# A gate branch through DRAM, the last convolution taps in a later stage, a fused mask and row maximum, and a plain unit between keys and values

## The chip, the cores and the metric

The kernel runs on one core of one Trainium2 chip. The metric is device time in microseconds (us) of one execution, the median of several runs; lower is better. The engines are named as in the profile: PE multiplies matrices (PEld loads its weights), DVE and ACT work on vectors, POOL is used here for small work and for issuing DMAs, and SP issues the DMAs of the weights. PE writes to PSUM, which has eight banks; everything else lies in SBUF or in DRAM. Each engine works through its own queue in order.

## The reference

One decoder layer on 256 tokens with 2048 channels, in float32. Two mixers run side by side on the same normalised input: causal attention with 16 heads on compressed queries, keys and values, and a short convolution over three tokens. Each is widened by a SiLU gate and projected back; the two are merged by sigmoid gates and projected once more.

```python
h = _rmsnorm(x, pre_norm_g)
(q_a, c_kv, k_rope, z_mla, c_in, b_gate, c_gate, z_conv, g_mla, g_conv) = split(h @ w_in)
q = _rmsnorm(q_a) @ w_q_b ; k_nope, v = split(_rmsnorm(c_kv) @ w_kv_b)   # 16 heads, rope on q and k
attn = softmax(causal(q k) * scale) v
y_mla = (attn * silu(z_mla)) @ w_o_mla
u = c_gate * c_in
conv = sum(conv_w[k] * u_pad[:, k:k + s] for k in range(3))
y_conv = (b_gate * conv * silu(z_conv)) @ w_o_conv
merged = sigmoid(g_mla) * y_mla + sigmoid(g_conv) * y_conv
out = x + _rmsnorm(merged @ w_out, post_norm_g)
```

The normalisation of x is taken out of the products: they run on x times its gain, and a factor r per token (`r_col`) is applied where a result leaves PSUM.

## The kernel before, in words

**Splitting.** To keep float32 accuracy every operand is split in a high part, rounded to the fast matmul type, and a low part, the remainder; a product is then three matmuls (`product`, L252: high by high, high by low, low by high). Weights come as units of 1 MB (128 partitions x 2048 values) into three `raw` buffers (SP issues them, L159). `split_unit` (L168) splits a unit: ACT writes the high part `whi` (L268), DVE subtracts it and writes the low part `wlo` (L269). There are three buffers of each. `take(i)` hands unit i to PE; `ahead` (L227) splits one unit further and loads three further. All units stand in one list, `plan` (L108 to L147), in the order in which PE takes them; the order of the attention stage is written out by hand twice, once for the list (L127 to L139) and once in the loop over the heads (L834 to L881), and both must agree.

**Order of the stages on PE.** First the compressed queries and keys (`qa`, `ckv`, `kr`). Then the attention stage: a loop over 16 heads, with 48 plain units (`fill`, L699) laid between the heads' steps. A plain unit is 24 matmuls of 128x512; four of them make one 512-wide column block of c_gate, c_in or z_mla (`cv` in PSUM), in the order of FILLS (L1157). Per group of two heads there is a key group "a" (`group_a`, L581: PE makes `qn` and `kn`, `whole`, L418, adds the two halves of a bank into `f`, and this is split) and a rope group "r"; per four heads there is one value group "v" (`group_v`, L601, `vv` in PSUM). The banks tagged "mm" are four, and qn, kn, qr and vv take them in turn, so a vv product waits until the `f` of an older one has been read out. At heads 5, 9 and 13 (`h > 1 == at`, the second head of a four) the order on PE is: scores, a plain unit, the key group, the value group, a plain unit, the values of the head before.

**Softmax** (`scores`, L616). The scores stand in one bank. DVE adds two halves (L636) and the causal mask (L637 and L638), takes the row maxima (L643), ACT takes the exponentials, DVE scales them and transposes 32x32 blocks; the rest of the transposition goes through DRAM by POOL's DMAs (`turned`, L344: `go` writes in four transfers, `come` reads back).

**The convolution taps** (`taps`, L750). Once a column block j of u = c_gate * c_in is done (L714, in `cv_f`), a generator works on it in three steps: POOL's DMAs bring copies shifted by one and two tokens (`mv`) and the rows of conv_w spread over the partitions (`cw`); DVE multiplies and adds (L758), first for the second half of the tokens, then for the first. Its steps are taken at `step()` (L737) in the loop over the heads; the last block, j = 3, takes them at the end of the attention stage.

**The gate blocks** (`block`, L913). Eight blocks of eight units compute z_conv (blocks 0 and 1), b_gate (2 and 3), g_mla (4 and 5) and g_conv (6 and 7); BLOCKS (L1158) gives the order. A unit is "whole", 8 products of 3 matmuls, or "pair". A pair takes two row blocks k and k + 4, both token halves and both column halves as a 2 x 2 by 2 x 2 block product with 7 products in place of 8. For this DVE and ACT make sums of the weights and split these too (`split_pair`, L202); the sums on the side of x are made once (`token_sums`), for three pairs. PLACES (L1159) says at which of the eight unit positions of each block a pair stands. At a block's end four results leave PSUM: for z_conv a sum and a SiLU into `cv_w`; for b_gate (`b_done`, L978) a sum and a multiplication by r and `cv_w`, in place; for the merge gates (`g_done`, L989) a sum, a sigmoid and a DMA to DRAM (`gate_far`), from where they are read back when they are needed.

**The projections** (`tokens`, L1029). Two products of 16 units each, first of the attention branch and then of the convolution branch, and then the output product of 16 units (`out`). During the first one `channels_steps(i)` (L1014) runs with unit i: it multiplies one 128x512 tile of the convolution by the tile of `cv_w` (L1020), starts its transposition, brings back the one of two steps before, and splits that of five steps before into `cv_both`, the operand of the second projection.

`tc.keep_in_program_order` pins an operation behind the operation traced before it on its engine; other operations may be moved in an engine's queue when the program is built.

Of the kernel before, what the change touches and what calls it, by code (L numbers as in the profile page):

```python
# [11 lines left out]
F32 = mybir.dt.float32  # L12
# [72 lines left out]
def tile_layer(ctx: ExitStack, tc: tile.TileContext, xw, x, pos, pvec, post_g, wc, wz, wcv, wkr, wqk, wqr, wv, cwr, wsq, wg, out):  # L85
# [43 lines left out]
    for h in range(H):  # L129
        at = h % HV  # L130
        order += ["fill"] + made[h] + [("v", h // HV)] * (h > 1 == at) + ["fill"] * (1 + (h > 0 and not h > 1 == at))
    for u in order:
# [483 lines left out]
    def scores(h):  # L616
# [19 lines left out]
        nc.vector.tensor_tensor(p[:, :P], sc[:, :P], half[:, :], op=ALU.add)  # L636
        nc.vector.tensor_tensor(p[:, :P], p[:, :P], mask[:, :P], op=ALU.add)  # L637
        nc.vector.tensor_tensor(p[:, P:], sc[:, S:], mask[:, P:], op=ALU.add)  # L638
        mx, sm, rs = temp("mx", (P, NT)), temp("sm", (P, NT)), temp("rs", (P, NT))
        nb = temp("nb", (P, NT))  # L640
        for t in range(NT):
            o = slice(t * P, (2 * t + 1) * P)
            nc.vector.reduce_max(mx[:, t : t + 1], p[:, o], axis=mybir.AxisListType.X)  # L643
        nc.vector.tensor_scalar(nb[:, :], mx[:, :], -SCALE, None, op0=ALU.mult)
# [54 lines left out]
    def fill(between=None):  # L699

        f = len(filled)
        filled.append(f)
        (j, n), i = FILLS[f // 4], f % 4
        if i == 0:
            cv_ps["now"] = [bank(f"cv{f}_{t}", tag="cv", bufs=2) for t in range(NT)]
        quarter(cv_ps["now"], take(u_fill[f]), i, between)
        if i < 3:
            return
        for t in range(NT):
            ps, r, u = cv_ps["now"][t], r_col[:, t : t + 1], cv_t[:, j, t, :]  # L710
            if n == 0:
                nc.scalar.activation(u, ps[:, :], AF.Copy, scale=r)
            elif n == 1:
                nc.vector.scalar_tensor_tensor(u, ps[:, :], r, u, op0=ALU.mult, op1=ALU.mult)  # L714
            else:
                nc.scalar.activation(z_now[:, t, :], ps[:, :], AF.Silu, scale=r)
        if n == 1:
            steps = taps(j)
            tap_steps.extend([steps] * 3 if j == 3 else [steps, None, steps, None, steps])
        elif n == 2:  # L720
            z_steps.append(gates_turn())
# [27 lines left out]

    def taps(j):  # L750

# [7 lines left out]

        cws = [temp("cw", (P, 512), bufs=3)[:, :] for _ in range(3)]  # L760
        for t in (1, 0):
            u, parts = cv_t[:, j, t, :], []
            for d in (1, 2):
                m = temp(f"mv{d}", (P, 512), bufs=1, tag=f"mv{d}x")
                if t:
                    bring(m[:d, :], cv_t[P - d :, j, 0, :])
                else:
                    tc.keep_in_program_order(nc.gpsimd.memset(m[:d, :], 0.0))
                bring(m[d:, :], u[: P - d, :])
                parts.append(m[:, :])  # L770
# [63 lines left out]
    for h in range(H):  # L834
# [3 lines left out]
        if h < H - 1:  # L838
            score(h)
        if h:  # L840
            fill()
# [5 lines left out]
        step()  # L847
        for i in made[h]:
            make(*i)
        if h > 1 == at:  # L850
            make("v", v)
            pt = turn(ps_by_head.pop(h - 1))
        if h == H - 3:
            lstack.close()
            d0 = dstack.enter_context(tc.tile_pool(name="d0", bufs=1))
            sums = token_sums(d0)
            xs = next(sums)
# [119 lines left out]

    def b_done(b):  # L978
        def done(ps, other, t, half):
            o = D // 2 * b + 512 * half  # L980
            w = spool["w"][:, t, o : o + 512]
            nc.vector.tensor_tensor(other, ps, other, op=ALU.add)
            nc.vector.scalar_tensor_tensor(w, other, r_col[:, t : t + 1], w, op0=ALU.mult, op1=ALU.mult)

        return done

    gate_far = {}

    def g_done(n, b):  # L989
        def done(ps, other, t, half):  # L990
            c = 2 * b + half
            g = spool["pool"].tile([P, 512], F32, name=f"sg{n}{c}{t}", tag="sg", bufs=4)
            nc.vector.tensor_tensor(g[:, :], ps, other, op=ALU.add)
            nc.scalar.activation(g[:, :], g[:, :], AF.Sigmoid, scale=r_col[:, t : t + 1])
            gate_far[n, c, t] = dram.tile([P, 512], F32, name=f"gate{n}{c}{t}", tag=f"gate{n}{c}{t}", bufs=1)
# [5 lines left out]
    for n, (name, b) in enumerate(BLOCKS):  # L1001
        put = g_done(*divmod(b, 2)) if name == "g" else {"zc": zc_done, "b": b_done}[name](b)
        if n == len(BLOCKS) - 1:
# [7 lines left out]

    channels_come = {}

    def channels_steps(i):  # L1014

        if i < 8:
            j, t = divmod(i, NT)
            u = cv_t[:, j, t, :]
            w = spool["w"][:, t, 512 * j : 512 * j + 512]
            tc.keep_in_program_order(nc.vector.tensor_tensor(u, u, w, op=ALU.mult))  # L1020
            go, channels_come[i] = turned(u, spool["pool"].tile([P, 512], F32, name="via_c", tag="via", bufs=2)[:, :], 4)
            go()
# [135 lines left out]
BLOCKS = [("zc", 0), ("zc", 1), ("b", 0), ("b", 1), ("g", 0), ("g", 1), ("g", 2), ("g", 3)]  # L1158
PLACES = [(4,), (0, 2, 4), (0, 2, 4), (0, 3), (0, 3)] + [(0, 2, 4)] * 3  # L1159

# [117 lines left out]
```

## Time and profile before

| | us |
|---|---|
| median of 3 runs | 1027.55 (1026.85 to 1028.34) |
| the profiled execution | 1027.61 |
| its span | 1025.6 |
| DVE, busy | 777.9 |
| ACT, busy | 536.5 |
| POOL, busy | 191.5 |

How to read it: the span runs from the first to the last instruction, and the execution's own time has a little more around it. The profile's page gives the busy time of each engine and the costliest groups of instructions. A line number such as L269 is one of kernel.py and can be that of a helper, so that one line stands for many places. In a row of a group the numbers behind the bar are the busy time of all its instructions in us, the mean of one in ns, and the idle time of the engine just before them with what ended it. The chain that ended last gives start, length and what was done. In a row of the windows, engines stand in the order PE, PEld, DVE, ACT, POOL, with their instructions in brackets, then the granted clock of PE, the share of the DMA engines and what they moved. In a timeline the number before an engine's name is a length, and the bracket at the end is the engine's idle time before it and what it waited for.

By the chain, PE starts its first matmul at 9.78 us, the loop over the heads ends at 422.13, the eight gate blocks end at 756.73, the two projections at 930.81, and the output product follows.

### The profile page before, as it was taken

The numbers are of one execution on the slowest core, as the hardware profiler recorded it, in microseconds if no ns is written. First come the engines' busy times: TensorE is split into PE (matmuls) and PEld (weight loads), VectorE is DVE, ScalarE is ACT, GpSimd is POOL, SyncE is SP. The second block draws the span as 40 slices with busy tenths as digits, with TensorE's granted clock in tenths as the row PEclk, the third lists the DMA queues.
The fourth block names the chain that finished last, engine by engine and source line by source line (L and its number), as shares of the span: only waits on it lengthen the run. The fifth ranks groups of instructions, "written<-read, shape, count | busy, mean of one in ns | idle before, by whom it ended". The sixth has DMA issues, their size and how long they took to land.

```text
span 1025.6 us, 12524 instructions
## 1 busy us (share of the span) xinstructions
PE 1014.0 (99%) x4634; PEld 844.6 (82%) x4634; DVE 777.9 (76%) x972; ACT 536.5 (52%) x667; POOL 191.5 (19%) x365
## 2 busy tenths in 40 slices
PE   9999999999999999999999999999999999999996
PEld 7888888788888888888888888888888888888885
DVE  7578787887879887898888788898877655656562
ACT  7756655565566664545544446555653433344451
POOL 7630321331213222220000000000024301322000
PEclk9999999999999999999999999999999999999999
DMA  8755684677666765775565556666678856777742
GB/s 324 303 192 199 227 250 180 218 249 260 222 221 202 259 217 199 259 246 212 184 216 197 202 205 221 231 237 217 234 258 300 312 217 211 271 267 243 310 165 82
DMA packets 43548, 236.25 MB, mean 230 GB/s; under 512 B 7840, under 2 KB 8544, under 8 KB 20576
## 3 DMA queue, kind: packets, MB, share of 16 engines
q1 hardware_dynamic: 29808, 197.54, 53.9%
q0 software_dynamic: 13248, 34.63, 10.7%
q10 hardware_dynamic: 432, 3.29, 0.8%
q8 instruction: 36, 0.59, 0.2%
q14 instruction: 24, 0.20, 0.1%
HBM read 215.53 MB, written 15.73 MB: 225 GB/s over the span
## 4 chain that ended last, share of the span: by engine, by line
PE 98%; DMA 1%; DVE 1%; ACT 0%; SPq 0%; issue 0%; DVEq 0%
PE g L90 33%; PE cv L90 26%; PE sq L90 17%; PE out L90 8%; PE vv L90 2%; PE kn L90 2%; PE qn L90 2%; PE ckv L90 2%; PE qa L90 2%; PE sc L90 1%; PE qr L90 1%; PE o L90 1%; DMA raw<-xw_dram 1%; PE kr L90 0%; DVE og L1132 0%; SPq L159 0%
## 5 line engine op out<-in xcount | busy, mean ns | idle before, releaser
L269 DVE TENSOR_TENSOR wlo<-raw,whi 128x1024 fp32r<-128x1024 f32 (+2 forms) x238 | 375.3, 1595 | 162.5 <-ACT whi L268 161.8
L268 ACT ACTIVATE whi<-raw 128x1024 fp32r<-128x1024 f32 (+2 forms) x240 | 316.6, 1346 | 296.9 <-PE sq L90 95.2
L90 PE MATMUL g<-whi,x_both 128*128 128x512 f32 x784 | 251.2, 389 | 0.0
L90 PE MATMUL cv<-whi,x_both 128*128 128x512 f32 x768 | 242.9, 390 | 0.0
L90 PEld LDWEIGHTS g<-whi,x_both 128*128 128x128 f32 x784 | 147.1, 188 | 30.4
L90 PEld LDWEIGHTS cv<-whi,x_both 128*128 128x128 f32 x768 | 144.2, 188 | 29.4
L90 PE MATMUL g<-wlo,x_both 128*128 128x512 f32 x392 | 152.5, 389 | 0.0
L90 PE MATMUL cv<-wlo,x_both 128*128 128x512 f32 x384 | 149.7, 390 | 0.0
L355 POOL DMA_DIRECT2D far<-via x96 | 52.8, 556 | 213.7 <-DVE via L348 160.0
L90 PEld LDWEIGHTS g<-wlo,x_both 128*128 128x128 f32 x392 | 73.6, 188 | 15.4
L90 PEld LDWEIGHTS cv<-wlo,x_both 128*128 128x128 f32 x384 | 72.2, 188 | 13.9
L90 PE MATMUL sq<-whi,x_both 128*128 128x512 f32 x256 | 79.0, 389 | 0.0
L90 PE MATMUL sq<-whi,cv_both 128*128 128x512 f32 x256 | 79.0, 389 | 0.0
L90 PE MATMUL out<-whi,x_both 128*128 128x512 f32 x256 | 79.0, 389 | 0.0
L996 POOL DMA_DIRECT2D gate<-sg x16 | 8.7, 542 | 306.3 <-PE g L90 185.0
L212 ACT ACTIVATE whi<-raw 128x1536 fp32r<-128x1536 f32 x20 | 29.8, 1491 | 61.7 <-PE g L90 44.4
L90 PEld LDWEIGHTS sq<-whi,x_both 128*128 128x128 f32 x256 | 48.0, 188 | 10.1
L90 PEld LDWEIGHTS sq<-whi,cv_both 128*128 128x128 f32 x256 | 48.0, 188 | 10.1
L90 PEld LDWEIGHTS out<-whi,x_both 128*128 128x128 f32 x256 | 48.0, 188 | 10.0
L210 DVE TENSOR_TENSOR wlo<-raw,whi 128x2048 fp32r<-128x2048 f32 x20 | 45.8, 2292 | 7.5 <-ACT whi L216 7.5
L90 PE MATMUL sq<-wlo,x_both 128*128 128x512 f32 x128 | 49.8, 389 | 0.0
L90 PE MATMUL sq<-wlo,cv_both 128*128 128x512 f32 x128 | 49.8, 389 | 0.0
(239 smaller groups left out, 1394.6 us busy)
## 6 DMA issues: line engine op xcount, KB each, us to landing
raw<-wg_dram SPq DMA_DIRECT2D x64, 1024.0 KB, 4.8
raw<-wsq_dram SPq DMA_DIRECT2D x48, 1024.0 KB, 5.2
raw<-wcv_dram SPq DMA_DIRECT2D x32, 1024.0 KB, 5.1
raw<-wz_dram SPq DMA_DIRECT2D x16, 1024.0 KB, 4.9
raw<-wqk_dram SPq DMA_DIRECT2D x8, 1024.0 KB, 4.8
raw<-wc_dram SPq DMA_DIRECT2D x4, 1024.0 KB, 10.0
raw<-wv_dram SPq DMA_DIRECT2D x4, 1024.0 KB, 4.8
gate<-sg POOLq DMA_DIRECT2D x16, 256.0 KB, 2.7
```

The source lines that it names most:

```text
L90: return tc.keep_in_program_order(nc.tensor.matmul(*a, **kw))
L210: tc.keep_in_program_order(nc.vector.tensor_tensor(*a, op=op))
L212: nc.scalar.activation(hi[:, 512:], t[:, 512:], AF.Copy)
L268: a = nc.scalar.activation(hi, src, AF.Copy)
L269: b = nc.vector.tensor_tensor(lo, src, hi.bitcast(F32), op=ALU.subtract)
L355: tc.keep_in_program_order(nc.gpsimd.dma_start(out=f[i], in_=m))
L996: tc.keep_in_program_order(nc.gpsimd.dma_start(out=gate_far[n, c, t][:, :], in_=g[:, :]))
```

## The change

- **b_gate.** `b_done` goes. The sums of blocks 2 and 3 leave as those of the merge gates do, without the sigmoid, to DRAM. In the first projection `branch_tile(i)` reads them back one step ahead (two buffers), and `channels_steps` multiplies each tile of the convolution by b_gate and r before it multiplies by `cv_w`.
- **Last taps.** The taps of column block 3 are no longer taken in the loop over the heads, but at steps 0, 2 and 4 of the first projection, with buffers of their own.
- **Mask and maximum.** One operation adds the mask and takes the row maximum.
- **Keys, plain unit, values.** At heads 5, 9 and 13 the key group comes before the first plain unit and the value group behind it; the list of units has the same order. `step()` comes behind that key group.
- **PLACES.** Blocks 3 and 4 have three paired units each in place of two.

```diff
@@ the list of units
-        order += ["fill"] + made[h] + [("v", h // HV)] * (h > 1 == at) + ["fill"] * (1 + (h > 0 and not h > 1 == at))
+        if h > 1 == at:
+            order += made[h] + ["fill", ("v", h // HV), "fill"]
+        else:
+            order += ["fill"] + made[h] + ["fill"] * (1 + (h > 0))
@@ scores
-        nc.vector.tensor_tensor(p[:, :P], p[:, :P], mask[:, :P], op=ALU.add)
-        nc.vector.tensor_tensor(p[:, P:], sc[:, S:], mask[:, P:], op=ALU.add)
-        for t in range(NT):
+        for t, src in enumerate((p[:, :P], sc[:, S:])):
             o = slice(t * P, (2 * t + 1) * P)
-            nc.vector.reduce_max(mx[:, t : t + 1], p[:, o], axis=mybir.AxisListType.X)
+            nc.vector.tensor_tensor_reduce(p[:, o], src, mask[:, o], 1.0, MASKED, ALU.add, ALU.max, mx[:, t : t + 1])
@@ fill
-            steps = taps(j)
-            tap_steps.extend([steps] * 3 if j == 3 else [steps, None, steps, None, steps])
+            steps = taps(j, bp) if j < 3 else None
+            if j < 3:
+                tap_steps.extend([steps, None, steps, None, steps])
@@ taps: its buffers come from the pool that is handed in
-    def taps(j):
+    def taps(j, pool):
-        cws = [temp("cw", (P, 512), bufs=3)[:, :] for _ in range(3)]
+        cws = [pool.tile([P, 512], F32, name=f"cw{d}", tag="cw", bufs=3)[:, :] for d in range(3)]
-                m = temp(f"mv{d}", (P, 512), bufs=1, tag=f"mv{d}x")
+                m = pool.tile([P, 512], F32, name=f"mv{d}", tag=f"mv{d}x", bufs=1)
@@ the loop over the heads
         if h < H - 1:
             score(h)
+        if h > 1 == at:
+            make(*made[h][0])
         if h:
             fill()
...
         step()
-        for i in made[h]:
-            make(*i)
         if h > 1 == at:
             make("v", v)
             pt = turn(ps_by_head.pop(h - 1))
+        else:
+            for i in made[h]:
+                make(*i)
@@ the ends of the gate blocks (b_done is deleted)
             nc.vector.tensor_tensor(g[:, :], ps, other, op=ALU.add)
-            nc.scalar.activation(g[:, :], g[:, :], AF.Sigmoid, scale=r_col[:, t : t + 1])
+            if n != "b":
+                nc.scalar.activation(g[:, :], g[:, :], AF.Sigmoid, scale=r_col[:, t : t + 1])
-        put = g_done(*divmod(b, 2)) if name == "g" else {"zc": zc_done, "b": b_done}[name](b)
+        put = zc_done(b) if name == "zc" else g_done("b", b) if name == "b" else g_done(*divmod(b, 2))
@@ ahead of the first projection
-    channels_come = {}
+    channels_come, b_come = {}, {}
+
+    def branch_tile(i):
+        w = spool["pool"].tile([P, 512], F32, name=f"b{i}", tag="b", bufs=2)
+        tc.keep_in_program_order(nc.gpsimd.dma_start(out=w[:, :], in_=gate_far[("b", *divmod(i, NT))][:, :]))
+        b_come[i] = w[:, :]
+
+    branch_tile(0)
+    tp = main.enter_context(tc.tile_pool(name="tp", bufs=1))
+    last_taps = taps(3, tp)
@@ channels_steps(i)
+        if i < 7:
+            branch_tile(i + 1)
+        if i in (0, 2, 4):
+            next(last_taps)
         if i < 8:
             j, t = divmod(i, NT)
-            u = cv_t[:, j, t, :]
+            u, r = cv_t[:, j, t, :], r_col[:, t : t + 1]
             w = spool["w"][:, t, 512 * j : 512 * j + 512]
+            tc.keep_in_program_order(nc.vector.scalar_tensor_tensor(u, b_come.pop(i), r, u, op0=ALU.mult, op1=ALU.mult))
             tc.keep_in_program_order(nc.vector.tensor_tensor(u, u, w, op=ALU.mult))
@@
-PLACES = [(4,), (0, 2, 4), (0, 2, 4), (0, 3), (0, 3)] + [(0, 2, 4)] * 3
+PLACES = [(4,)] + [(0, 2, 4)] * 7
```

More of the change, by code (lines that the diff above doesn't have):

```diff
@@ L976, in zc_done @@
         return done
[L978 to L985, printed above, removed]
     gate_far = {}
```

## The prediction

> **What bounds the kernel now.** I read the page first, then the waits of PE, then the chain of work that ended last in order of time, and after that the other engines stage by stage. The page gives the engines' shares, and PE's only wait inside the kernel's steady part follows it:
>
> ```profile
> PE 1014.0 (99%) x4634; PEld 844.6 (82%) x4634; DVE 777.9 (76%) x972; ACT 536.5 (52%) x667; POOL 191.5 (19%) x365
> ```
> ```profile
> PE vv L90 <- DVE f L422: 2.2, 2, 1.9
> ```
>
> PE works for nearly the whole span, so it sets the time and only two things can shorten it: fewer matmuls, or the removal of that 2.2 us. DVE at 76% is next, but its share is an average; where it runs full it can make PE wait. The same chain in order of time (start, length, what) shows both the price of a matmul and where PE lost time:
>
> ```profile
> 197.89 2.70 PE kn L90 x16
> 201.08 1.11 DVE wlo L269
> 202.19 0.34 DVE f L422
> 202.57 5.75 PE vv L90 x24
> 208.33 5.44 PE cv L90 x24
> ...
> 285.49 2.79 PE kn L90 x16
> 288.29 5.47 PE vv L90 x24
> 293.75 5.44 PE cv L90 x24
> ...
> 370.92 2.70 PE kn L90 x16
> 379.75 5.44 PE cv L90 x24
> ...
> 422.13 334.60 PE g L90 x1476
> 756.73 174.08 PE sq L90 x768
> ```
>
> From the last two rows: 334.60 / 1476 and 174.08 / 768 are both 0.2267 us for a 128x512 matmul, without a pause in the eight gate blocks ("g") or in the two projections ("sq"). In the other rows the values' matmuls ("vv") follow a group's keys ("kn") three times. From the start of kn to the start of the plain unit behind vv PE took 208.33 - 197.89 = 10.44 us at head 5, 293.75 - 285.49 = 8.26 us at head 9, and 379.75 - 370.92 = 8.83 us at head 13. Head 9 is undisturbed: 2.79 + 5.47 us. Heads 5 and 13 lost 2.18 and 0.57 us, together 2.75 us (more than the 2.2 us of the wait, since PE also restarts its pipeline). At head 5 the chain runs through DVE in these microseconds: a weight split (wlo, L269) stands in DVE's queue ahead of the sum f (L422) that empties the bank which vv is to take.
>
> **Part 1: two more paired units.** PLACES gives blocks 3 and 4 three paired units each in place of two. A paired unit has 7 products of 3 matmuls, a whole one 8 of 3, so 2 x 3 = 6 matmuls go: 6 x 0.2267 = 1.36 us of PE time. The bytes from DRAM stay the same. The price is paid by DVE:
>
> ```profile
> L269 DVE TENSOR_TENSOR wlo<-raw,whi 128x2048 fp32r<-128x2048 f32 x92 | 210.5, 2289 | 120.5 <-ACT whi L268 120.1
> L210 DVE TENSOR_TENSOR wlo<-raw,whi 128x2048 fp32r<-128x2048 f32 x20 | 45.8, 2292 | 7.5 <-ACT whi L216 7.5
> L210 DVE TENSOR_TENSOR tlo<-tf,thi 128x1536 fp32r<-128x1536 f32 x20 | 35.1, 1753 | 1.1 <-ACT thi L217 1.1
> L210 DVE TENSOR_TENSOR tf<-raw 128x1024 f32<-128x1024 f32 x20 | 24.4, 1218 | 0.0
> L210 DVE TENSOR_TENSOR tf<-raw 128x512 f32<-128x512 f32 x20 | 13.8, 692 | 0.7
> L210 DVE TENSOR_TENSOR raw<-raw,tf 128x512 f32<-128x512 f32 x20 | 13.8, 689 | 0.4
> ...
> L348 DVE STREAM_TRANSPOSE via_c<-cv_f 128x512 f32<-128x512 f32 x8 | 5.6, 703 | 0.0
> ...
> L983 DVE SCALAR_TENSOR_TENSOR cv_w<-u,r_both,cv_w 128x512 f32<-128x512 f32 x6 | 4.1, 746 | 0.0
> ```
> ```profile
> 500.00:525.00 25.00, 25.00 (x112) 20.71 (x111) 23.01 (x18) 15.09 (x13) 0.00 (x0) 1.00 0.57 202
> ...
> 750.00:775.00 25.00, 25.00 (x112) 20.71 (x111) 17.45 (x18) 13.19 (x11) 9.20 (x17) 1.00 0.76 277
> 775.00:800.00 25.00, 25.00 (x112) 20.71 (x111) 19.57 (x19) 10.03 (x9) 13.21 (x25) 1.00 0.87 302
> ```
>
> A whole unit costs DVE 2.29 us, a paired one 2.29 + 1.75 + 1.22 + 0.69 + 0.69 = 6.64. A block with three pairs asks for 5 x 2.29 + 3 x 6.64 = 31.4, and some eight sums of about 0.69 us at its ends (5.5): 36.9 us of DVE, against 183 x 0.2267 = 41.5 us of PE. That is 89%, and the cover is 4.6 us a block. Blocks 1, 2, 5, 6 and 7 have this form already, and the 500 to 525 window, at the seam of blocks 1 and 2, has DVE at 23.01 of 25 with PE still at 25.00. Block 3 runs the ends of block 2, and there the change also takes away the four scalar_tensor_tensor of 0.746 us (L983), so blocks 3 and 4 come out like 5 and 6. I count no loss. If the cover were gone, each paired unit could cost up to its surplus over the whole one, 4.35 us.
>
> **Part 2: the plain unit between keys and values.** At heads 5, 9 and 13 the key group moves ahead of the head's first plain unit, so that unit lies between kn and vv: 24 x 0.2267 = 5.44 us in which the sums f can empty the banks. The largest wait was 1.9 us, so it is covered nearly three times. The step of the convolution and gate helpers, whose sums also stood in DVE's queue at head 5, now comes behind the key group. Gain 2.75 us; bounds 0 (if the queue of DVE keeps f as late as before, or another wait takes the place) and 2.75. What is late next is the split of the unit behind vv, which has a plain unit's time in hand as before. I take 2.75, since head 9 shows the sequence without loss even without the unit between.
>
> **Part 3: mask and maximum in one.** Per head, these go:
>
> ```profile
> L638 DVE TENSOR_TENSOR p<-sc,mask 128x256 f32<-128x256 f32 x16 | 6.6, 415 | 0.0
> L643 DVE TENSOR_REDUCE mx<-p 128x1 f32<-128x256 f32 x16 | 6.6, 412 | 0.0
> L637 DVE TENSOR_TENSOR p<-p,mask 128x128 f32<-128x128 f32 x16 | 4.5, 283 | 0.1
> L643 DVE TENSOR_REDUCE mx<-p 128x1 f32<-128x128 f32 x16 | 4.4, 276 | 0.0
> ```
>
> Two fused operations take their place. No row shows one. If it runs at the pace of the addition alone, a head saves 0.412 + 0.276 = 0.69 us of DVE; if it takes as long as both, nothing; if it is slower than both, say by the same 0.69, that much is lost. All of it lies on DVE beside PE's work, where only a stage with a wait feels it, and the only such waits go with part 2. On the path: 0, either way. I take the first value, because the reductions' times are those of one pass over the row.
>
> **Part 4: b_gate through DRAM, last taps moved.** In blocks 2 and 3, 8 multiplications leave and 8 DMAs of 256 KB are issued on POOL, which did nothing at all around there (0.00 in the 500 to 525 row); nothing is queued behind them. From the end of the attention 10 sums and products of the taps (0.69 us each, as the 128x512 rows of part 1), 9 DMAs and 2 memsets leave; PE did not wait there, so 0. All of this comes back in the first 43.5 us of the first projection (8 steps of 24 x 0.2267 = 5.44 us from 756.73): 8 x 0.746 + 10 x 0.69 = 12.9 us of DVE, 8 loads, 9 DMAs and 2 memsets on POOL. The two windows from 750 to 800 had DVE at 17.45 + 19.57 = 37.0 of 50, so it becomes 49.9 of 50: full. What saves PE is how early the splits are made:
>
> ```profile
> 767.70 1.92 ACT L268 ACTIVATE whi<-raw 128x2048 fp32r<-128x2048 f32 x1 [3.52 <-PE sq L90]
> ```
> ```profile
> 753.30 2.29 DVE L269 TENSOR_TENSOR wlo<-raw,whi 128x2048 fp32r<-128x2048 f32 x1
> 755.50 0.69 DVE L1020 TENSOR_TENSOR cv_f<-cv_f,cv_w 128x512 f32<-128x512 f32 x1
> 758.77 2.29 DVE L269 TENSOR_TENSOR wlo<-raw,whi 128x2048 fp32r<-128x2048 f32 x1 [0.19 <-ACT whi L268]
> 769.65 2.29 DVE L269 TENSOR_TENSOR wlo<-raw,whi 128x2048 fp32r<-128x2048 f32 x1 [2.54 <-ACT whi L268]
> ```
>
> ACT's part of a split begins when PE gives back one of the three buffers. The one at 767.70 belongs to the unit that PE takes at 756.73 + 4 x 5.44 = 778.5, and DVE ends its part at 769.65 + 2.29 = 771.9. So a split may be 6.5 us late before PE feels it. DVE's queue is in order, and the new product (b tile, r, u) waits for a DMA. What is queued behind it is the next split, and behind that PE. The rows for the DMA, in this stretch, and POOL's queue ahead of it:
>
> ```profile
> gs<-gate POOLq DMA_DIRECT2D x8, 256.0 KB, 7.3
> ```
> ```profile
> 759.64 1.77 POOL L996 DMA_DIRECT2D gate<-sg  x3 [4.66 <-ACT sg L994]
> 761.40 0.54 POOL L1054 DMA_DIRECT2D gs<-gate  x1
> ```
> ```profile
> L355 POOL DMA_DIRECT2D far<-via_c x32 | 17.5, 554 | 18.5 <-DVE via_c L348 11.0 <-DVE cv_both L269 3.1 <-DMA far<-via_c 2.6
> ```
> ```profile
> cw<-cwr_dram POOLq DMA_DIRECT2D x12, 256.0 KB, 8.3
> gate<-sg POOLq DMA_DIRECT2D x16, 256.0 KB, 2.7
> ```
>
> The first b tile can be issued behind the last gate tile, at 761.4, and lands at about 761.4 + 7.3 = 768.7. A split that stands behind its product, its multiplication and its transpose (0.75 + 0.69 + 0.70, by L983, the 128x512 rows and L348) begins at 770.8. Later each step's chain on POOL is one landing (7.3), these 2.1 us on DVE, four transfers out and one back (5 x 0.55 = 2.75), for two steps, since two b tiles are in flight: (7.3 + 2.1 + 2.75) / 2 = 6.1 us against PE's 5.44. In quiet stretches a 256 KB transfer of this kind took 2.7 us (the last row), which gives 3.8 us. I expect DVE to fall behind by some 2 to 5 us over these steps, inside the 6.5, and to catch up after the eighth step. Cost 0 in the likeliest case; bounds 0 and the 9.6 us of the rival below.
>
> The Trainium skill, page "DMA: Bandwidth & Descriptors", section "Anatomy of one DMA — SWDGE (gpsimd) path", gives about 2.0 us and bytes / 436e3 for one such DMA, 2.6 us for 256 KB by its figures. The quiet gate writes (2.7) agree with it and the loads of this stretch (7.3) do not; by the rule POOL's loop would be far faster than PE's steps and the rival below would have hardly a chance, so the traced landing is the one to use.
>
> **Sum.** The profiled execution took 1027.61 us (span 1025.6), 0.06 above the median of the runs, 1027.55. 1027.61 - 1.36 - 2.75 = 1023.5 us. A measurement here can tell about 0.2%, 2.05 us, from no change.
>
> **Rivals.** (a) DVE's queue makes PE wait in the first projection. In the trace of before each step's product stands directly behind the split traced ahead of it and ahead of the next (755.50, between the wlo of 753.30 and 758.77). If that order is kept, the split of the third unit begins at 770.8 and ends at 773.1, while PE wants its low part at 756.73 + 2 x 5.44 + 0.45 = 768.1: 5.0 us of wait. With the 6.5 us used up, the next seven steps run at POOL's 6.1 us: 7 x 0.66 = 4.6 more. 1023.5 + 9.6 = 1033.1 us, slower than before. It decides the sign from 4.1 us of waiting on. The order and the landing speak for it; against it, the queue need not keep that order, and a b tile that is known to arrive late would be queued behind the splits that are ready. Half of it, about 4 us, would give 1027.5. (b) Part 2 does not do what it says: f stays late in DVE's queue, or a bank, a split or the scores wait instead. The time is then 1027.61 - 1.36 = 1026.25 us. Against it stands the 5.44 us cover. (c) The raw weights land late: the DMA engines were busy 0.87 of 775 to 800, and about 3.8 MB more come (8 b tiles, 4 tap tiles, 3 rows spread over the partitions). But the weights are issued three buffers ahead, and this would only add to (a); I put it there.
>
> **How the numbers follow.** Forecast, with up to 2 us of waiting in the projection: 0.62, its own range 1022.6 to 1025.5. Rival (a) in full or mostly: 0.18 (slower by over 0.2%); about half of it: 0.10 (within 0.2%). Rival (b): 0.10 (within 0.2%). So faster 0.62, same 0.20, slower 0.18. The range goes from 1022.6 (the forecast and the spread of 0.8 us that the runs show) to 1030.5, which leaves out the worst part of (a), about 0.12, and 0.06 below.
>
> **What would show it.** Right: 1470 matmuls of g in 333.2 us; no wait of vv on f; kn, a plain unit and vv back to back at heads 5, 9 and 13; in the first projection 384 matmuls in 87.0 us. Wrong: waits of sq on wlo with a DMA of the b tile, the mv or the cw tiles behind them in the 40 us after the last block; DVE rows of the fused operation well over 0.7 us; waits of g in blocks 3 and 4; or a new wait ahead of the moved key group.

## The result, and the profile after

The changed kernel takes 1023.44 us, median of 6 runs (1023.06 to 1023.56); the kernel before took 1027.39 in 6 runs beside them (1026.85 to 1029.08). The ratio is 0.9956, its 95% interval 0.9945 to 0.9966: faster by 0.4%. The forecast was 1023.5. The profiled execution took 1023.56, its span is 1021.8.

In the changed kernel the lines have moved: L272 is the low part of a weight (L269 before), L213 what a paired unit adds (L210), L425 the sum f (L422), L644 the fused mask and maximum, L760 the taps, L1013 the DMA that brings a b tile, L1030 the new product and L1031 the multiplication by `cv_w` behind it.

PE's waits of the changed kernel, all of them (us in total, times, longest), both in the first 10 us:

```profile
PE idle L90 <- POOL hpi L295: 1.1, 1, 1.1
PE qa L90 <- ACT whi L271: 0.5, 1, 0.5
```

The wait of vv on f is gone, and no other took its place. The chain that ended last, in order of time (start, length, what):

```profile
77.38 2.77 PE qn L90 x16
...
192.65 2.79 PE kn L90 x16
195.44 5.47 PE cv L90 x24
200.91 5.44 PE vv L90 x24
206.34 5.44 PE cv L90 x24
...
419.58 333.24 PE g L90 x1470
752.82 174.08 PE sq L90 x768
926.90 87.05 PE out L90 x384
```

At head 5 kn, a plain unit, vv and the next plain unit stand back to back. From the first qn to the start of g it is 419.58 - 77.38 = 342.20 us, against 422.13 - 77.19 = 344.94 before: -2.74. The eight gate blocks take 333.24 against 334.60: -1.36. Both projections and the output product have the lengths that they had, 174.08 and 87.05. The start of the kernel took 0.19 more. That is all there is: -2.74 - 1.36 + 0.19 = -3.91 us at the end of the output product, of which the span shows 3.8.

The fused operation, in the groups by form (busy us, mean ns of one):

```profile
L644 DVE CUSTOM_DVE_ANT_0 p<-sc,mask 128x256 f32<-128x256 f32 x16 | 6.7, 417 | 0.0
L644 DVE CUSTOM_DVE_ANT_0 p<-p,mask 128x128 f32<-128x128 f32 x16 | 4.6, 289 | 0.1
L644 DVE DVE_READ_ACCUMULATOR2_ANT mx<- 128x1 f32 x32 | 2.8, 86 | 0.0
```

It runs at the pace of the addition alone (417 and 289 ns, against 415 and 283), but each brings a second instruction of 86 ns that reads the maximum out. A head costs 417 + 289 + 2 x 86 = 878 ns in place of 1386: 0.51 us saved.

The stage that could have lost it, the first projection, by windows (PE, PEld, DVE, ACT, POOL; granted clock, DMA share, GB/s) and then in DVE's queue:

```profile
750.00:775.00 25.00, 25.00 (x112) 20.72 (x111) 19.25 (x19) 11.17 (x11) 11.94 (x22) 1.00 0.92 316
775.00:800.00 25.00, 25.00 (x112) 20.72 (x111) 22.64 (x25) 10.38 (x7) 12.65 (x24) 1.00 0.88 312
```

```profile
754.88 2.29 DVE L272 TENSOR_TENSOR wlo<-raw,whi 128x2048 fp32r<-128x2048 f32 x1 [1.32 <-ACT whi L271]
760.30 2.29 DVE L272 TENSOR_TENSOR wlo<-raw,whi 128x2048 fp32r<-128x2048 f32 x1 [1.93 <-ACT whi L271]
762.51 0.74 DVE L1030 SCALAR_TENSOR_TENSOR cv_f<-b,r_both,cv_f 128x512 f32<-128x512 f32 x1
...
788.19 0.69 DVE L760 TENSOR_TENSOR cv_f<-cv_f,cw 128x512 f32<-128x512 f32 x1 [2.15 <-DMA mv<-cv_f]
...
790.63 2.25 DVE L272 TENSOR_TENSOR wlo<-raw,whi 128x2048 fp32r<-128x2048 f32 x1
```

PE stays at 25.00 of 25. DVE had 19.25 + 22.64 = 41.9 us to do in these 50, not the 49.9 that I had put there: the eight products begin 7.85 us apart, (817.46 - 762.51) / 7, so the last ones fall behind 800. The first product begins at 762.51 without waiting: the splits of 754.88 and 760.30 stand ahead of it, two that stood behind the first product in the kernel before. The taps wait once for 2.15 us on a DMA (788.19), and the split at 790.63 stands behind them. It ends at 792.9; it is that of the ninth unit, which PE takes at 752.82 + 8 x 5.44 = 796.3. That is the closest call: 3.4 us were left.

### The profile page after: what moved, and what is told of

It reads as the page before. It is cut to its first block, busy times and chain, and to the rows that moved or that the text cites. A ratio compares the mean times of both kernels' runs of the same rounds, so it can differ in the third digit from the quotient of the medians.

```text
span 1021.8 us, 12570 instructions
## 1 busy us (share of the span) xinstructions
PE 1012.2 (99%) x4628; PEld 843.7 (83%) x4628; DVE 778.7 (76%) x980; ACT 540.2 (53%) x671; POOL 200.9 (20%) x381
## 3 DMA queue, kind: packets, MB, share of 16 engines
q10 hardware_dynamic: 432, 3.29, 0.8%
## 4 chain that ended last, share of the span: by engine, by line
PE 98%; DMA 1%; DVE 0%; ACT 0%; SPq 0%; issue 0%; DVEq 0%
PE g L90 33%; PE cv L90 26%; PE sq L90 17%; PE out L90 9%; PE kn L90 2%; PE qn L90 2%; PE vv L90 2%; PE ckv L90 2%; PE qa L90 2%; PE sc L90 1%; PE qr L90 1%; PE o L90 1%; DMA raw<-xw_dram 1%; PE kr L90 0%; DVE og L1143 0%; SPq L162 0%
## 5 line engine op out<-in xcount | busy, mean ns | idle before, releaser
L272 DVE TENSOR_TENSOR wlo<-raw,whi 128x1024 fp32r<-128x1024 f32 (+2 forms) x236 | 370.8, 1588 | 148.4 <-ACT whi L271 147.6
L271 ACT ACTIVATE whi<-raw 128x1024 fp32r<-128x1024 f32 (+2 forms) x238 | 313.2, 1343 | 274.3 <-PE sq L90 90.1
L90 PE MATMUL g<-whi,x_both 128*128 128x512 f32 x760 | 244.9, 389 | 0.0
L90 PEld LDWEIGHTS g<-whi,x_both 128*128 128x128 f32 x760 | 142.7, 188 | 29.7
L90 PE MATMUL g<-wlo,x_both 128*128 128x512 f32 x380 | 147.8, 389 | 0.0
L90 PEld LDWEIGHTS g<-wlo,x_both 128*128 128x128 f32 x380 | 71.3, 188 | 14.7
L215 ACT ACTIVATE whi<-raw 128x1536 fp32r<-128x1536 f32 x22 | 32.8, 1493 | 70.1 <-PE g L90 45.8
L213 DVE TENSOR_TENSOR wlo<-raw,whi 128x2048 fp32r<-128x2048 f32 x22 | 50.4, 2292 | 8.8 <-ACT whi L219 8.8
L90 PE MATMUL out<-wlo,x_both 128*128 128x512 f32 x128 | 49.8, 389 | 0.0
```

Of the source, the lines that this page charges most:

```text
L90: return tc.keep_in_program_order(nc.tensor.matmul(*a, **kw))
L213: tc.keep_in_program_order(nc.vector.tensor_tensor(*a, op=op))
L215: nc.scalar.activation(hi[:, 512:], t[:, 512:], AF.Copy)
L271: a = nc.scalar.activation(hi, src, AF.Copy)
L272: b = nc.vector.tensor_tensor(lo, src, hi.bitcast(F32), op=ALU.subtract)
```

## The experiments

Six kernels start from the kernel before and take parts of the change, or from the changed kernel and undo parts. Then two disturb the first projection, three put more pairs into block 0, and one keeps b_gate on the chip in another way. A ratio is to the kernel before, in runs on the same chip.

### Only PLACES

```diff
-PLACES = [(4,), (0, 2, 4), (0, 2, 4), (0, 3), (0, 3)] + [(0, 2, 4)] * 3
+PLACES = [(4,)] + [(0, 2, 4)] * 7
```

> The kernel before with nothing changed but PLACES (three paired units in blocks 3 and 4). Theory: PE time is a count of matmuls, so g has 1470 in 333.2 us; with b_gate's multiplications still in the blocks' ends, block 3 asks for 36.8 + 4 x 0.75 = 39.8 us of DVE against 41.5 of PE, so it still fits: 1.36 us faster than before, no wait of g. Rival, that b_gate had to leave the blocks first: PE waits in blocks 3 and 4 for the splits, and the gain is gone or turned into a loss, up to 2 x 4.35 us.

Measured: 1031.29 us (8 runs, 1028.70 to 1031.74), ratio 1.0026 [1.0015, 1.0037]: slower. PE's waits, the one at the seam, and DVE's queue ahead of it:

```profile
PE g L90 <- DVE tlo L210: 2.7, 2, 1.4
PE vv L90 <- DVE f L422: 2.5, 2, 2.2
```

```profile
561.18 0.50 PE L90 MATMUL g<-tlo,xs 128*128 128x512 f32 x1 [1.37 <-DVE tlo L210]
```

```profile
549.33 0.74 DVE L983 SCALAR_TENSOR_TENSOR cv_w<-p,r_both,cv_w 128x512 f32<-128x512 f32 x1
...
552.38 2.07 DVE L983 SCALAR_TENSOR_TENSOR cv_w<-u,r_both,cv_w 128x512 f32<-128x512 f32 x3
...
554.98 2.28 DVE L210 TENSOR_TENSOR wlo<-raw,whi 128x2048 fp32r<-128x2048 f32 x1
557.18 2.28 DVE L269 TENSOR_TENSOR wlo<-raw,whi 128x2048 fp32r<-128x2048 f32 x1
559.38 1.75 DVE L210 TENSOR_TENSOR tlo<-tf,thi 128x1536 fp32r<-128x1536 f32 x1
```

PE waits for `tlo` of the second pair of block 3, and the same happens one block later. The four multiplications of `b_done` (L983, 0.74 + 2.07 us) stand between the ends of the last block and this split. The gate blocks take 760.13 - 423.55 = 336.58 us for 1470 matmuls, 3.34 over the 333.24 of the changed kernel and 1.98 over the kernel before. I had counted that these blocks fit, since their average would be 39.8 of 41.5 us; this fell. The average says nothing of the seam, where a paired unit's work and the last block's ends come at once. So b_gate had to leave the blocks before the pairs could be had. (In the profiled execution PE lost another 1.76 us earlier, 423.55 - 76.85 = 346.70 us from the first qn to g in place of 344.94. That is head 5, where the edit does nothing; the last section comes back to it.)

### Only the plain unit between keys and values

```diff
-        order += ["fill"] + made[h] + [("v", h // HV)] * (h > 1 == at) + ["fill"] * (1 + (h > 0 and not h > 1 == at))
+        if h > 1 == at:
+            order += made[h] + ["fill", ("v", h // HV), "fill"]
...
+        if h > 1 == at:
+            make(*made[h][0])
         if h:
             fill()
...
```

> The kernel before with the plain unit between a group's keys and the values at heads 5, 9 and 13 alone. Theory: the wait of vv on f goes, 2.75 us faster than before, heads 5, 9 and 13 alike, g still 334.6 us. Rival, that the wait went because the fused operation and the moved taps gave DVE room: some of the wait at head 5 stays, the gain is under 1.5 us.

Measured: 1024.52 us (5 runs, 1024.12 to 1024.98), ratio 0.9963 [0.9951, 0.9976]. No wait of vv is left, and the chain has

```profile
419.26 334.60 PE g L90 x1476
```

From the first qn, at 77.07, to g it is 342.19 us, 2.75 less than before; g keeps its 334.60. This term is shown by itself.

### Only the fused operation, and the change without the unit

```diff
-        nc.vector.tensor_tensor(p[:, :P], p[:, :P], mask[:, :P], op=ALU.add)
-        nc.vector.tensor_tensor(p[:, P:], sc[:, S:], mask[:, P:], op=ALU.add)
...
+            nc.vector.tensor_tensor_reduce(p[:, o], src, mask[:, o], 1.0, MASKED, ALU.add, ALU.max, mx[:, t : t + 1])
```

> The kernel before with mask and row maximum in one operation alone. Theory: DVE saves 0.5 us a head (two fused operations and two accumulator reads for four operations), none of it on the path: the wait of vv at head 5 changes by less than 0.7 us, the time is that of before within 0.7 us. Rival: the saved DVE time is what f waited for; the wait of 2.2 us goes, up to 2.75 us faster.

The second kernel is the changed one with the old order at heads 5, 9 and 13:

```diff
-        if h > 1 == at:
-            order += made[h] + ["fill", ("v", h // HV), "fill"]
+        order += ["fill"] + made[h] + [("v", h // HV)] * (h > 1 == at) + ["fill"] * (1 + (h > 0 and not h > 1 == at))
...
```

> The changed kernel with the old order at heads 5, 9 and 13 (key group and value group side by side); everything else of the change stays. Theory: the wait of vv on f comes back, 2.75 us slower than the changed kernel, 1.36 us faster than the one before. Rival, DVE's room through the fused operation: at most 0.7 us of the wait comes back, 3.3 us or more faster than before.

Measured: the fused operation alone 1026.72 us (11 runs, 1025.98 to 1028.63), ratio 0.9987 [0.9979, 0.9996]; the change without the unit 1025.21 (6 runs, 1024.39 to 1025.78), 0.9967 [0.9955, 0.9979]. Their waits of vv, first of the one and then of the other:

```profile
PE vv L90 <- DVE f L422: 1.5, 1, 1.5
```

```profile
PE vv L90 <- DVE f L422: 1.8, 1, 1.8
```

In both one wait is left, that of head 5; the small one of head 13 is gone. From the first qn to g it is 421.25 - 77.21 = 344.04 us in the first, 0.90 less than before, and 421.49 - 77.17 = 344.32 in the second, 2.12 more than in the changed kernel (I had expected 2.75). So the fused operation isn't worth nothing in the old order. What these traces show of it is head 13: from kn to the plain unit behind vv PE took 8.83 us in the kernel before, 8.87 with PLACES alone and 8.87 in the next experiment, and 8.32 and 8.36 in the two kernels with the fused operation, which is 0.5 us less. The other 0.4 of the 0.90, at head 5, can't be put down to it: the wait there differs as much between kernels whose edits lie nowhere near it (1.90 us in the kernel before, 1.06 in the next experiment, which is 0.81 us shorter from the first qn to g). Behind the unit, where f has time, the operation is worth nothing: the two together give 2.74, no more than the unit alone.

### Only b_gate and the last taps; the taps put back

The first kernel is the kernel before with `b_done` deleted, the sums of blocks 2 and 3 to DRAM, the b tiles and the last taps in the first projection. The second is the changed kernel with

```diff
-            steps = taps(j, bp) if j < 3 else None
-            if j < 3:
-                tap_steps.extend([steps, None, steps, None, steps])
+            steps = taps(j, bp)
+            tap_steps.extend([steps] * 3 if j == 3 else [steps, None, steps, None, steps])
...
-        if i in (0, 2, 4):
-            next(last_taps)
```

> The kernel before with b_gate through DRAM and the last taps in the first projection alone (old PLACES, old order of the heads, mask and maximum apart). Theory: 12.9 us of DVE work and 25 transfers come into the first projection, all inside the 6.5 us that a split may be late: no wait of sq, the time of before within 0.7 us. Rival, that the work costs where it lands: sq waits for wlo, slower than before by some us, which in the whole change would have been hidden by another gain.

> The changed kernel with the last taps back in the loop over the heads; b_gate still goes through DRAM. Theory: the taps cost nothing in either place, since PE waits in neither, so the time is that of the changed kernel within 0.7 us, and in the first projection DVE and POOL get 6.9 us and 11 instructions less. Rival, that the taps in front of block 0 would make PE wait at the end of the attention or in block 0: a wait of cv or g between 400 and 440, 1 us or more slower.

Measured: 1027.56 us (12 runs, 1026.35 to 1030.33), ratio 1.0005 [0.9997, 1.0014], with sq at 174.08 unbroken: the move costs nothing and gains nothing by itself. The taps put back: 1023.49 (5 runs, 1023.25 to 1023.75), against 1023.44 with them moved, and no wait of PE in either place. In the first projection DVE has 19.61 + 18.96 = 38.6 us to do from 750 to 800 without the taps, 41.9 with them; the room isn't needed.

### The rival's order, forced

The rival of the prediction put each step's product ahead of the next splits. Here the splits of the first projection's units are pinned in the order in which they were traced, which keeps that order:

```diff
-            split_act(hi[:, h:e], lo[:, h:e], t[:, h:e])
+            split_act(hi[:, h:e], lo[:, h:e], t[:, h:e], pin=u_d[0][0][1] < i <= u_d[0][2][3])
...
+        if pin:
+            tc.keep_in_program_order(b)
```

> The changed kernel, but in the first projection the low part of each weight split (units 2 to 11) is pinned on DVE behind all that was traced before it, so that step i of the convolution stands ahead of the split of unit i + 2. This is the order that the rival of the prediction supposed. Theory: it was the order of DVE's queue that kept PE from waiting. With the first b tile landing at about 762 the third unit's split ends at 767 or later, while PE wants it at 764: 2 to 5 us of wait at the start, then little more: 2 to 6 us slower than the changed kernel. The rival's own price: 9.6 us slower. A third way: the order does not matter and the time is that of the changed kernel.

Measured: 1036.68 us (4 runs, 1035.92 to 1037.03), ratio 1.0090 [1.0075, 1.0104]. PE's waits, the first and the longest of them, DVE's queue ahead of the longest, and PE's clock around it:

```profile
PE sq L90 <- DVE wlo L272: 9.3, 3, 6.4
```

```profile
765.26 0.50 PE L90 MATMUL sq<-wlo,x_both 128*128 128x512 f32 x1 [1.20 <-DVE wlo L272]
...
782.84 0.80 PE L90 MATMUL sq<-wlo,x_both 128*128 128x512 f32 x1 [6.41 <-DVE wlo L272]
```

```profile
760.81 0.75 DVE L1032 SCALAR_TENSOR_TENSOR cv_f<-b,r_both,cv_f 128x512 f32<-128x512 f32 x1 [2.77 <-DMA b<-gateb]
...
772.13 0.69 DVE L762 TENSOR_TENSOR mv<-mv,cw 128x512 f32<-128x512 f32 x1 [1.34 <-DMA cw<-cwr_dram]
...
778.39 0.75 DVE L1032 SCALAR_TENSOR_TENSOR cv_f<-b,r_both,cv_f 128x512 f32<-128x512 f32 x1 [1.45 <-DMA b<-gateb]
...
780.53 4.45 DVE L272 TENSOR_TENSOR wlo<-raw,whi 128x2048 fp32r<-128x2048 f32 x2
```

```profile
780.00:784.00 4.00, 1.16 (x3) 0.97 (x4) 4.00 (x3) 1.33 (x1) 3.10 (x6) 0.50 0.34 82
784.00:788.00 4.00, 4.00 (x11) 3.13 (x10) 3.93 (x6) 0.00 (x0) 0.20 (x1) 0.50 0.97 346
```

The product waits 2.77 us for the first b tile and 1.45 for a later one, the taps 1.34 for a row of conv_w, and the split at 780.53 stands behind all of them. The two projections take 940.06 - 752.96 = 187.1 us, 13.0 more than 174.08: 9.3 of waits, some 3.0 behind the 6.4 us pause, where the clock was at half (0.50 in both rows; the 27 matmuls from 782.84 to 791.91 took 9.07 us in place of 6.12), and the restarts behind the two other waits. I had expected 2 to 6 us here after seeing the result, and the prediction 9.6; both left out the clock. The two kernels do the same work and differ in the pinned order alone: it is the order in DVE's queue that keeps PE going in the changed kernel.

### More work on DVE in each step

Two multiplications of 128x512 into a buffer that nobody reads are added to each of the eight steps of the changed kernel:

```diff
+            for _ in range(2):
+                extra = tp.tile([P, 512], F32, name="extra", tag="extra", bufs=1)
+                tc.keep_in_program_order(nc.vector.tensor_tensor(extra[:, :], w, w, op=ALU.mult))
             tc.keep_in_program_order(nc.vector.tensor_tensor(u, u, w, op=ALU.mult))
```

> The changed kernel with two more 128x512 multiplications on DVE in each of the eight steps of the first projection (their result is not used): 16 x 0.6 = 10 us or more. Theory: the splits were at most 2.8 us late of 6.5 (the one at 790.63 ends 3.9 us ahead of PE), so about 3.9 us more are free and the rest, some 4 to 6 us, becomes a wait of sq on wlo, unless the queue lets the splits pass: 0 to 6 us slower. Rival, that DVE has room in this stage anyway: no wait, same time, and the margin of the splits unchanged.

Measured: 1032.23 us (6 runs, 1029.70 to 1033.75), ratio 1.0046 [1.0033, 1.0059]. The profiled execution, 1029.7, is the shortest of them. It has one wait of PE, at the start of the second projection, 839.8 to 844.3; that wait, and what DVE did in it:

```profile
PE sq L90 <- DVE at_f L1079: 4.5, 1, 4.5
```

```profile
842.87 0.69 DVE L272 TENSOR_TENSOR cv_both<-cv_f,cv_both 128x512 fp32r<-128x512 f32 x1 [3.00 <-ACT cv_both L271]
843.48 1.28 DVE L1079 TENSOR_TENSOR at_f<-sq,gs 128x512 f32<-128x512 f32 x2
```

The 384 matmuls behind it take 88.70 us in place of 87.04, with the clock at 0.59 from 844 to 848; 4.5 + 1.7 is the whole 6.1 us of this span over that of the changed kernel. That is the top of the 0 to 6 us that I had expected; the median, 8.8 us over the changed kernel, lies above them. The five longer executions have a mean clock of 0.993 to 0.995 against 0.997 in this one, and its trace can't say where they lost it. The place was not the expected one: here no split came late. The channel steps themselves ended too late: the last tile came back from DRAM, ACT's part of `cv_both` waited 4.67 us for it, DVE's 3.00 for ACT's, and the sums that empty PE's banks (`at_f`) stood behind that. What is late next in this stage, as far as this execution shows, is the loop of steps over POOL and DRAM, and not the weights.

### More pairs in block 0

```diff
-PLACES = [(4,)] + [(0, 2, 4)] * 7
+PLACES = [(0, 2, 4)] * 8
...
+PLACES = [(2, 4)] + [(0, 2, 4)] * 7
...
+PLACES = [(2, 4, 6)] + [(0, 2, 4)] * 7
```

> The changed kernel with three paired units in block 0 too, in place of one: 6 matmuls fewer. The last taps have left the stretch from 425 to 450, where DVE is now at 17.57 of 25. Theory: 1.36 us faster than the changed kernel, g 1464 matmuls in 331.9 us, provided that the sums on the side of x are ready for a pair at unit 0. Rival: the first pair comes while DVE still ends the attention; PE waits in block 0 for its split, same or slower.

> The changed kernel with two pairs in block 0, at units 2 and 4, in place of one at 4. The pair at unit 0 cost a wait of 9.1 us, since its split stood behind the end of the attention on ACT and DVE; a pair at 2 is split two units later. Theory: no wait, 3 matmuls fewer, 0.68 us faster than the changed kernel, g 1467 matmuls in 332.6 us. Rival: DVE is still behind at that time and PE waits ahead of unit 2, slower.

> The changed kernel with three pairs in block 0, at units 2, 4 and 6. Theory: as with two, and the third pair at unit 6 still leaves unit 7 and 4.35 us of surplus ahead of block 1's first pair: 6 matmuls fewer, 1.36 us faster than the changed kernel. Rival: the third pair's split meets block 1's first two (units 0 and 2) and DVE falls behind; a wait of g of 1 to 5 us at the seam of blocks 0 and 1, same or slower.

Measured, in this order: 1032.32 us (5 runs, 1032.11 to 1033.41), ratio 1.0052 [1.0040, 1.0064]; 1026.63 (11 runs, 1025.27 to 1026.98), 0.9986 [0.9978, 0.9995]; 1034.31 (5 runs, 1032.44 to 1035.42), 1.0067 [1.0054, 1.0080]. All three are slower than the changed kernel, where I had expected them to be faster by 1.36, 0.68 and 1.36 us. The waits of the second, its DVE queue and the clock behind the wait:

```profile
PE g L90 <- DVE tlo L213: 2.2, 1, 2.2
```

```profile
422.21 0.71 DVE L351 STREAM_TRANSPOSE via<-z_now 128x512 f32<-128x512 f32 x1 [3.29 <-ACT z_now L717]
...
428.59 2.28 DVE L272 TENSOR_TENSOR wlo<-raw,whi 128x2048 fp32r<-128x2048 f32 x1
430.79 1.75 DVE L213 TENSOR_TENSOR tlo<-tf,thi 128x1536 fp32r<-128x1536 f32 x1
```

```profile
430.00:435.00 5.00, 2.77 (x8) 1.94 (x7) 4.90 (x5) 1.92 (x2) 0.08 (x1) 0.79 0.92 375
435.00:440.00 5.00, 5.00 (x21) 4.00 (x20) 3.25 (x3) 2.45 (x3) 0.00 (x0) 0.87 0.46 161
```

From 422.21 DVE has no pause, and `tlo` still ends at 432.5 while PE wants it at 430.4. Ahead of 422.21, though, DVE stood idle for 3.29 us, more than the 2.23 that PE lost: the pair's sums (from 423.77 on) stand in its queue behind a transposition that waits for ACT's `z_now`, a gate of the attention branch. Their weights had landed, since ACT splits them at 418.68. So it may again be the order of the queue and not the amount of work; no run puts the sums ahead. The gate blocks end at 755.89, 3.07 us later than in the changed kernel, though a further pair saves 0.68 (3 matmuls): the wait of 2.2 and the clock of 0.79 and 0.87 after it cost more. In the first kernel PE waits twice, 3.7 us for ACT's `thi` and 4.0 for `tlo`, and the clock falls to 0.50; in the third 7.4 us in two waits for `tlo`.

### b_gate kept on the chip, its multiplications later

The kernel before with the unit, the fused operation and the new PLACES; `b_done` keeps its sums in SBUF, and the four multiplications are taken at units 5, 6 and 7 of the next block:

```diff
-            nc.vector.tensor_tensor(other, ps, other, op=ALU.add)
-            nc.vector.scalar_tensor_tensor(w, other, r_col[:, t : t + 1], w, op0=ALU.mult, op1=ALU.mult)
+            nc.vector.tensor_tensor(g[:, :], ps, other, op=ALU.add)
+            later.append((w, g[:, :], r_col[:, t : t + 1]))
...
+        jobs = {5: [multiply], 6: [multiply] * 2, 7: [multiply]} if name == "b" else {}
```

> The kernel before with the new order of the heads, the fused operation and three pairs in blocks 3 and 4, but b_gate kept on the chip: at a block's end only its four sums are made (into the buffers that the merge gates use later), and the four multiplications by r and cv_w follow behind the next block's pairs (units 5 to 7). The taps stay in the attention stage. Theory: what made the pairs impossible was the 2.8 us of multiplications at the seam ahead of the second pair's split, not the sum of DVE's work; with the same work a few units later no wait of g is left, g 1470 matmuls in 333.2 us, the time of the changed kernel within 0.7 us, and the first projection as in the kernel before. Rival: a block's DVE work (39.8 of 41.5 us) is itself too much, g waits in blocks 3 and 4 as with PLACES alone, 3 us or more slower than the changed kernel.

Measured: 1024.63 us (9 runs, 1024.21 to 1024.92), ratio 0.9973 [0.9963, 0.9983]. PE's wait:

```profile
PE g L90 <- DVE tlo L213: 0.8, 2, 0.4
```

The gate blocks take 753.98 - 419.33 = 334.65 us, 1.41 over the 333.24, where the same multiplications at the seam cost 3.34; I had expected no loss here. So more than half of the loss was their place. Whether the rest is their amount or the new place isn't separated; off the blocks altogether is the best of the three.

## Why the prediction was right

The time and both terms of the sum were right. The unit alone gives 2.75 us; the two pairs give 1.36 in every kernel with them whose trace has no wait of g (333.24 against 334.60), and alone they lose. That the time agrees to 0.06 us is partly luck: the 2.75 was read from one execution of the kernel before, whose own runs lie 2.2 us apart.

**Part 1** was right for the changed kernel, and for the reason given at its end, that the multiplications of L983 leave. The reckoning by the block's share (89%) was weaker than it looked: with PLACES alone the same reckoning gives 96%, and PE waits at two seams.

**Part 2** was right in its mechanism too. In DVE's queue of the kernel before, and then of the changed one:

```profile
199.91 0.68 DVE L758 TENSOR_TENSOR cv_f<-cv_f,mv 128x512 f32<-128x512 f32 x1
...
201.01 1.18 DVE L269 TENSOR_TENSOR wlo<-raw,whi 128x1024 fp32r<-128x1024 f32 x1
202.11 0.74 DVE L422 TENSOR_TENSOR f<-qn,half 128x256 f32<-128x256 f32 x2
```

```profile
193.17 0.42 DVE L425 TENSOR_TENSOR f<-qn,half 128x256 f32<-128x256 f32 x1
193.71 0.42 DVE L425 TENSOR_TENSOR f<-qn,half 128x256 f32<-128x256 f32 x1
...
200.94 0.42 DVE L425 TENSOR_TENSOR f<-kn,half 128x256 f32<-128x256 f32 x1
```

The f that vv waits for is that of qn (that of kn, at 200.94 in the changed kernel, comes when vv has begun). Before, qn ended at 197.89 and its f was taken 4.2 us later, behind the last of the taps' products and two splits, of which the second is shown; PE wanted the bank at 200.59, 2.7 us after qn. Now f is taken 0.5 us after the end of qn at 192.65, and PE wants the bank only 8.3 us after it, at 200.91. Both the unit between and the place ahead of the taps help. By these numbers the first alone would do, since an f that came 4.2 us behind qn again would still be 3 us early, but no run has it without the second.

**Part 3** was off twice without harm. "On the path: 0, either way" holds behind part 2 only; in the old order the operation saves 0.5 us at head 13, and at head 5 the traces can't tell. And its saving is 0.51 us a head, not 0.69, for the reads of the maximum.

**Part 4** came out at 0 as said, with DVE behind by as much as 3.1 of the 6.5 us that it had (2 to 5 were expected). Its inner numbers were less good: a step takes 7.85 us, not 6.1. With the taps back in the loop over the heads it takes (812.19 - 763.81) / 7 = 6.9, so the taps' DMAs and waits are about half of what I left out. A b tile lands in 7.3 us as assumed, but as a median, in the DMA view from 746 to 806:

```profile
b<-gateb POOLq DMA_DIRECT2D x7, 256.0 KB, 7.3
```

The first one, issued at 756.89, landed after 5.0 us and was there when the product was taken at 762.51. **Rival (a)** described a real mechanism whose order didn't come about. That its price of 9.6 us is near what the waits of the pinned kernel add up to, 9.3, is luck. It put 5.0 us at the third unit, with the first b tile landing after 7.3 us; there the tile took 3.8 and PE waited 1.20. The large wait, 6.41, came two units later, behind the taps and a later b tile, where the rival had 0.66 us a step. The time is still 1036.7 and not 1033.1, since it left out what the pauses do to the clock.

## What to carry to other kernels

A stage's share of an engine doesn't show whether one more job fits; look at the few microseconds in which its jobs come at once, here the seam of two blocks. Work that waits for a DMA cost nothing or 13 us here by its place in an engine's queue, so ask what stands behind it before asking how long it takes. Independent matmuls between a product and the reuse of its bank hide what several small savings on the vector engine would buy one by one, and those savings then are worth nothing more.

## What was not expected of the hardware

A pause of PE costs more than its length when it is long enough. Pauses of 1.90 us (the kernel before, head 5) and 1.79 (the change without the unit) left the granted clock at 1.00. One of 2.19 us in the same place, with PLACES alone, did not:

```profile
200.00:205.00 5.00, 2.81 (x9) 2.12 (x8) 5.00 (x8) 2.68 (x6) 3.69 (x8) 0.72 0.38 93
205.00:210.00 5.00, 5.00 (x23) 4.04 (x22) 2.75 (x8) 1.47 (x4) 1.09 (x3) 0.94 1.01 385
```

```profile
202.51 7.19 PE vv L90 x24
```

The values' 24 matmuls took 7.19 us in place of 5.75; that 1.44 and the longer wait, 0.3, are the 1.76 us that the edit can't explain. In the 4 or 5 us window behind a pause of 2.23 us the clock was 0.79 (two pairs in block 0), behind 4.5 us 0.59, behind 6.4 us 0.50. The Trainium skill, page "TensorE: Matmul & The Clock Gate", section "Why this matters for your kernels", asks for no idle gaps above some 3 us; here 2.2 us were too many already, and the measurement decides. That the kernel before scatters from 1026.65 to 1030.02 in 19 runs beside the first experiments, and the kernels without a pause at head 5 within 1 us (1024.12 to 1024.98, 1023.06 to 1023.56), would follow if its pause costs the clock in some executions and not in others. The mean granted clock of each execution fits: of those 19 the seven at 1029.04 us and above have 0.996, the twelve at 1027.90 and below 0.997 or 0.998. In the same way the kernel with two pairs at units 2 and 4 of block 0 has seven executions of 1026.44 to 1026.98 at 0.996 and four of 1025.27 to 1025.46 at 0.997 or 0.998. That the clock fell at head 5 in them is not shown: only one execution of each kernel was profiled.

A short wait costs more than the wait as well: vv takes 5.75 us after the pause of head 5 at full clock, and 5.47 or 5.44 without one.
